# Two fused blocks on one core: mixer operations of Vector with one operand in PSUM, a new order of heads, and a front in a fixed order

## Chip, cores, metric

One core of a Trainium2 chip runs the whole program. The metric is the device time in microseconds (us) of one execution. Five engines work in parallel, each with its own queue in program order: TensorE (PE, matrix products), Vector (DVE), Scalar (ACT), GpSimd (POOL) and SyncE (SP, which here issues most transfers). SBUF is the on-chip memory of the operands, PSUM the memory into which TensorE writes its products.

## What is computed

512 tokens of width 1024 go through two blocks, all in fp32. The first takes `h = rmsnorm(x) * (1 + scale) + shift`, where shift and scale come from a conditioning vector `c` ("ada"), projects h, runs 8 heads of stick-breaking attention and 8 of forgetting attention, and adds a gated output. The second is a mixer, a cross attention to 256 memory rows, and a feed-forward block with a convolution of 3 taps. What the change touches is the start of the program and the mixer, cut from the reference:

```python
def hybrid_mixer(h, ...):                       # second block
    q, k, v, u = split(h @ w_in)                # 4 heads, 2 maps of 64 per head
    q, k = partial_rope(q), partial_rope(k)     # the first 16 of 64 columns turn
    lam = exp(sum(lam_q1 * lam_k1)) - exp(sum(lam_q2 * lam_k2)) + lam_init
    # per head and block of 128 queries:
    p = softmax(where(mask, q @ k.T / 8, -inf)) # both maps
    a = (p[0] - lam * p[1]) @ v
    a = rmsnorm(a, subln_g) * (1 - lam_init)
    c = u[:, :512] * sigmoid(u[:, 512:])
    c = causal_dwconv(c, cv_dw_w) + cv_dw_b     # 31 taps, 512 channels
    c = silu(layernorm(c, cv_ln_g, cv_ln_b))
    return concat([a, c]) @ w_out

def cross_attention(h, m, w_cq, w_ckv, w_co):   # m = rmsnorm(mem, norm_mem_g)
    k, v = split(m @ w_ckv)
```

## The kernel before

Every weight comes in units of 128 x 1024 fp32 (512 KB): `load` (L137) has SyncE transfer it, `split` (L149) has Scalar cast it to a high part `wh` (L152), and Vector or GpSimd subtract that for a low part `wl` (L153); a string of letters D and P says which of the two engines. A product is three matmuls, high by high, high by low and low by high (`mm3`, L159). So a unit feeds 24 matmuls. Three units are buffered.

The order on the engines follows the order in which the program is written, kept by a scheduler that lets an instruction pass another where its model says that this one waits. The written order is in two strings. `FRONT` (L83) mixes the steps of the start: k0 to k7 and v0 to v3 are the products of the memory with `w_ckv` (16 units), n the memory's norm, o the step that multiplies a key product by the norm (L371) and writes it to DRAM (`kv_d`), x the loads of the tokens with their squares (summed by GpSimd into `xacc`, L427), r the norm of the tokens (`row_norm`, L429), a the eight conditioning pairs (`ada`, L409, two Vector operations of 128 x 1024 each), h the normed tokens (`token_h`, L434). Behind h7 come the first block's projections. Sums over the partitions of a column are matmuls with ones (`col_sums`, L238); a reciprocal root is a Scalar root, a Vector reciprocal and four small steps (`rsq_v`, L247); a row of such numbers is spread over the partitions by a cast (`bch`), a subtraction (`bcl`) and matmuls with the identity (`bcast_mm`, L278).

`MIX` (L98) orders the mixer: u is one quarter of the gated input of the convolution (`glu`, L809: two chunks of 24 matmuls), q one half of the heads' queries and keys with their rotation (`rotated`, L858: Scalar copies all columns out of PSUM, then six Vector operations on 64 columns each), v one half of the values, f the front of a head (`diff_front`, L902: scores of both maps, maxima, exponentials, the weighted difference L924), b its back (`diff_back`, L928: transposes, product with v, the head's norm by `rsq_bits`, L258), c one quarter of the convolution (`conv`, L952: 8 taps on TensorE, 14 on Vector in the PSUM bank `sm`, of which there is one, and 9 on Scalar and GpSimd), l the layer norm (L989). Then the output projection runs, first `wo2c` on the convolution (L1036), then `wo2a` on the heads (L1044).

## Time and profile before

| | |
|---|---|
| median of 3 runs | 1317.12 us (1312.56 to 1318.27) |
| the profiled execution | 1315.84 us, of it span 1314.0 |
| TensorE | busy 1229.4 us, 94% of the span |
| Vector | 803.5 us, 61% |
| Scalar | 611.8 us, 47% |
| GpSimd | 472.1 us, 36% |
| mean granted TensorE clock | 0.962 |

The span is what the engines' records cover; the execution lasts 1.84 us longer. A share is a mean over stages with different limits: the busy share of TensorE is near 100% in long stretches and much lower in a few, so the tables by stretch say more than the total. [...]

### The profile page before, as it was taken

The page shows a single profiled execution, that of the slowest core. Times are in us where ns is not written, and L with a number is a line of the kernel's source. Part 1 is how long each engine was busy: PE and PEld are TensorE (multiplying, and loading weights), DVE is VectorE, ACT ScalarE, POOL GpSimd, SP SyncE. Part 2 cuts the span into 40 slices and gives each one's busy share as a digit, 9 for nine tenths or more (in the row PEclk, how much of TensorE's full clock was granted, in tenths as well). Part 3 has the DMA queues.
Part 4 walks back from the last instruction along what each step waited for, and adds up shares of the span by engine and source line. Part 5 has one row for each costly group of instructions (what it writes and reads, how often), then busy time and mean ns, then how long its engine had stood idle before and what let it go on. Part 6 is the DMA issues. An engine that isn't in the chain of part 4 may idle for free.

```text
span 1314.0 us, 16828 instructions
## 1 busy us (share of the span) xinstructions
PE 1229.4 (94%) x6368; PEld 1036.9 (79%) x6368; DVE 803.5 (61%) x1221; ACT 611.8 (47%) x1001; POOL 472.1 (36%) x322
## 2 busy tenths in 40 slices
...
GB/s 362 228 201 124 81 96 73 65 78 92 65 137 257 129 133 98 80 84 94 67 55 41 16 32 144 84 61 48 109 86 101 100 98 99 98 89 88 89 88 65
DMA packets 43715, 135.91 MB, mean 103 GB/s; under 512 B 4977, under 2 KB 8561, under 8 KB 43634
## 3 DMA queue, kind: packets, MB, share of 16 engines
...
HBM read 125.38 MB, written 6.29 MB: 100 GB/s over the span
## 4 chain that ended last, share of the span: by engine, by line
PE 76%; DVE 13%; ACT 4%; issue 3%; DMA 2%; POOL 2%; SPq 0%; DVEq 0%; POOLq 0%; ACTq 0%
PE lin L134 66%; PE z L134 5%; DVE sm L976 2%; PE pv L134 2%; DVE wl L153 1%; PE z L533 1%; DMA wr<-in_wts 1%; DVE ar L413 1%; ACT wh L152 1%; DVE p L924 1%; DVE h L206 1%; POOL wl L153 1%; DVE nm L919 0%; PE sm L134 0%; ACT cpr L972 0%
## 5 line engine op out<-in xcount | busy, mean ns | idle before, releaser
L134 PE MATMUL lin<-h,wh 128*128 128x512 f32 (+1 forms) x2296 | 710.3, 390 | 8.4 <-ACT wh L152 7.9
L134 PEld LDWEIGHTS lin<-h,wh 128*128 128x128 f32 x2296 | 428.7, 191 | 93.3 <-ACT wh L152 10.2
L134 PE MATMUL lin<-h,wl 128*128 128x512 f32 (+1 forms) x1148 | 444.3, 388 | 6.1 <-DVE wl L153 4.4
L153 POOL TENSOR_TENSOR wl<-wr,wh 128x1024 fp32r<-128x1024 f32 (+1 forms) x110 | 268.0, 2436 | 484.0 <-ACT wh L152 455.2
L152 ACT CAST wh<-wr 128x1024 fp32r<-128x1024 f32 (+1 forms) x197 | 204.9, 1042 | 276.5 <-PE lin L134 207.8
L134 PEld LDWEIGHTS lin<-h,wl 128*128 128x128 f32 x1148 | 218.7, 191 | 50.0 <-DVE wl L153 5.6
L153 DVE TENSOR_TENSOR wl<-wr,wh 128x1024 fp32r<-128x1024 f32 (+1 forms) x87 | 115.6, 1328 | 139.8 <-ACT wh L152 139.0
L134 PE MATMUL lin<-wh,h 128*128 128x256 f32 x672 | 128.4, 288 | 2.0 <-ACT wh L152 1.1
L134 PEld LDWEIGHTS lin<-wh,h 128*128 128x128 f32 x672 | 108.0, 195 | 2.6 <-ACT wh L152 1.4
L1158 DVE SCALAR_TENSOR_TENSOR cv<-up,vecs,cv 128x512 f32<-128x512 f32 x88 | 94.5, 1074 | 17.9 <-ACT cv L1156 16.4
L134 PE MATMUL lin<-wl,h 128*128 128x256 f32 x336 | 96.5, 287 | 2.1 <-DVE wl L153 2.1
L134 PE MATMUL lin<-zz,wh 128*128 128x512 f32 (+1 forms) x324 | 92.4, 370 | 0.0
L134 PEld LDWEIGHTS lin<-wl,h 128*128 128x128 f32 x336 | 65.4, 195 | 2.6 <-DVE wl L153 2.4
L134 PEld LDWEIGHTS lin<-zz,wh 128*128 128x128 f32 x324 | 58.5, 188 | 11.4
L134 PE MATMUL lin<-zz,wl 128*128 128x512 f32 (+1 forms) x162 | 60.0, 370 | 0.0
L301 POOL TENSOR_TENSOR nacc<-nacc,sq 128x512 f32<-128x512 f32 x34 | 52.7, 1559 | 14.3 <-ACT sq L300 13.9
L1153 POOL MEMSET up<- 128x2 f32 x44 | 4.3, 99 | 148.8 <-DVE cv L1158 116.7
L604 POOL TENSOR_TENSOR zs<-zs,y 64x512 f32<-64x512 f32 x16 | 26.5, 1654 | 72.2 <-DVE y L603 69.9
L134 PE MATMUL z<-qk 128*128 128x512 f32 (+3 forms) x96 | 36.2, 377 | 8.2 <-ACT p L920 4.9
L976 DVE SCALAR_TENSOR_TENSOR sm<-cp,vecs,sm 128x512 f32<-128x512 f32 x56 | 42.0, 749 | 0.6
L1165 ACT ACTIVATE cv<-cv 128x512 f32<-128x512 f32 x22 | 13.9, 632 | 59.9 <-DVE cv L1158 59.9
L618 DVE TENSOR_TENSOR_SCAN om<-om 128x511 f32<-128x511 f32 (+3 forms) x32 | 36.7, 1187 | 8.2 <-ACT om L614 8.0
(371 smaller groups left out, 1739.4 us busy)
## 6 DMA issues: line engine op xcount, KB each, us to landing
wr<-in_wts SPq DMA_DIRECT2D x197, 512.0 KB, 3.5
...
```

The costliest lines, as they stand in the source:

```text
L134: pe.matmul(o, lhsT=lhsT, rhs=rhs, start=start, stop=stop, skip_group_check=True)
L152: act.copy(out=hi[:, :n], in_=raw[:, :n])
L153: lo_engine().tensor_tensor(out=lo[:, :n], in0=raw[:, :n], in1=f32(hi[:, :n]), op=ALU.subtract)
L206: dve.scalar_tensor_tensor(out=lo, in0=src, scalar=g, in1=f32(hi), op0=ALU.mult, op1=ALU.subtract)
L301: pool.tensor_tensor(out=acc, in0=acc, in1=q, op=ALU.add)
L413: dve.scalar_tensor_tensor(out=r, in0=r, scalar=1.0, in1=cb, op0=ALU.mult, op1=ALU.mult, accum_out=mod[:, 2 * j + n:2 * j + n + 1])
L533: pe.transpose(z[:, o + i * P:o + (i + 1) * P], pt[rb_][:, ro:ro + P], ident)
L604: pool.tensor_tensor(out=zs[r], in0=zs[r], in1=y[r], op=ALU.mult)
L618: dve.tensor_tensor_scan(out=om[:, o:e], data0=om[:, o:e], data1=om[:, o:e], initial=1.0, op0=ALU.mult, op1=ALU.bypass)
L976: dve.scalar_tensor_tensor(out=cz, in0=x_, scalar=w_, in1=cz, op0=ALU.mult, op1=ALU.add)
L1158: dve.scalar_tensor_tensor(out=r, in0=up[:, 2 - j:2 - j + T], scalar=V("ffn_w", c * 3 + j), in1=r, op0=ALU.mult, op1=ALU.add)
L1165: act.activation(out=a, in_=a, func=AF.Silu)
```

## The change

Five edits; the first and the last move instructions.

The front is written in a fixed order for all five engines (`manual_schedule`): a loop over the 16 memory units, each step of which splits unit n + 2, loads what the tables `ADA_LOADS`, `ADA_AT` and `NORM_AT` say, and runs unit n. `START_LO` gives each unit's engine for the low part. The memory's norm no longer scales the products in the front; its numbers (`mrc`, `mrb`) are kept, and the keys and values are scaled when the cross attention reads them back. A token's high and low part are made from a product that reads the norm from PSUM.

The rotation reads q and k from PSUM and leaves its products there, with the norm's factor multiplied into the sine and cosine tables ahead (eight small operations); Scalar copies only the 48 columns that do not turn. In a head's front the exponentials of map 0 go back into PSUM and the difference reads them there; in its back, the steps of the norm and the product with it work in PSUM. The row norm's broadcast `r1b` also stays in PSUM. The string `MIX` is another.

```diff
-START_LO = "DP"
+START_LO = "DDPPDPPDPPDPPDPP"
+ADA_LOADS = (2, 1, 1, 2, 1, 1, 2, 1, 1, 2, 1, 1)
+ADA_AT = (5, 5, 6, 7, 8, 8, 9, 10, 12, 12, 13, 14, 15, 15, 16, 16)
+NORM_AT = (8, 10)
-FRONT = ("k0 k1 n o0 o1 x0 k2 o2 x2 k3 o3 x4 x6 v0 a0 k4 o4 a1 k5 o5 r v1 a2 k6 o6 a3 k7 o7 h0 h1 a4 v2 h2 a5 a6 v3 "
-         "h3 h4 a7 h5 h6 h7")
-MIX = "u0 q0 f0 c0 u1 q1 f1 c1 v1 v0 u2 f3 b0 c2 u3 b1 c3 b3 f2 l b2"
+MIX = "q0 u0 f0 u1 f1 v0 c0 c1 b0 u2 b1 q1 u3 c2 f2 c3 v1 l f3 b2 b3"
...
-    def rsq_bits(o, v):
+    def rsq_bits(o, v, bank):
-        y, t, g = (smp.tile([P, 16], F32, tag="rq" + n, name="rq")[:, :w] for n in "ytg")
+        y = bank[:, 32:32 + w]
+        t, g = (smp.tile([P, 16], F32, tag="rq" + n, name="rq")[:, :w] for n in "tg")
...
-            dve.tensor_tensor(out=t, in0=y, in1=y, op=ALU.mult)
-            dve.tensor_tensor(out=t, in0=t, in1=g, op=ALU.mult)
+            dve.tensor_tensor(out=t, in0=y, in1=g, op=ALU.mult)
+            dve.tensor_tensor(out=t, in0=t, in1=y, op=ALU.mult)
...
+            return lambda: (act.copy(out=q[:, :NM], in_=o),
+                            nc.gpsimd.dma_start(out=kv_d[n // 4, :, (n % 4) * NM:(n % 4 + 1) * NM], in_=q[:, :NM]))
...
     def token_h(j):
-        xk = xt0[:, j]
-        dve.tensor_tensor(out=xk, in0=xk, in1=xrb, op=ALU.mult)
-        act.activation(out=xk, in_=xk, func=AF.Identity, scale=gain[:, j:j + 1], bias=shift[:, j:j + 1])
-        hs.append(split_sb(xk))
+        xk, sh = xt0[:, j], shift[:, j:j + 1]
+        dve.scalar_tensor_tensor(out=xk, in0=xk, scalar=gain[:, j:j + 1], in1=xrb, op0=ALU.mult, op1=ALU.mult)
+        hi, lo = htile(), htile()
+        act.activation(out=hi, in_=xk, func=AF.Identity, bias=sh)
+        dve.scalar_tensor_tensor(out=lo, in0=xk, scalar=sh, in1=f32(hi), op0=ALU.add, op1=ALU.subtract)
+        hs.append((hi, lo))
...
+    with tc.manual_schedule(engines={E_.PE, E_.Activation, E_.DVE, E_.Pool, E_.SP}):
...
+        mem_split(0)
+        load_x(6)
+        mem_split(1)
+        for n in range(17):
+            if n < 16:
+                mem_split(n + 2)
+            if n < len(ADA_LOADS):
+                for _ in range(ADA_LOADS[n]):
+                    ada_load()
+            if n == 0:
+                memory_squares()
+            if 1 <= n <= 4:
+                squares_x(2 * n - 2)
+                squares_x(2 * n - 1)
+            out_ = mem_unit(n) if n < 16 else lambda: None
+            if n == NORM_AT[0]:
+                rsq(xrc, col_sums([xacc]), D)
+                bcast_mm(xrc, xrb)
+            if n == NORM_AT[1]:
+                memory_norm()
+            for i in range(16):
+                if ADA_AT[i] == n:
+                    ada(i)
+                    if i % 2 and n > NORM_AT[0]:
+                        while 2 * len(hs) < i:
+                            token_h(len(hs))
+            out_()
...
-    bcast(r1c, rb[:, 1])
+    r1b = ps_pv()
+    bcast_mm(r1c, r1b)
...
+    for t in (cosb, sinb):
+        for i in range(NT):
+            dve.tensor_scalar(out=t[:, i], in0=t[:, i], scalar1=r12c[:, i:i + 1], scalar2=None, op0=ALU.mult)
...
+            og = o.rearrange("p (a g d) -> p a g d", a=2, d=64)
...
-            dve.tensor_tensor(out=ra, in0=t1, in1=cb, op=ALU.mult)
-            dve.tensor_tensor(out=rb_, in0=t2, in1=sb_, op=ALU.mult)
-            dve.tensor_tensor(out=rc, in0=t2, in1=cb, op=ALU.mult)
-            dve.tensor_tensor(out=rd, in0=t1, in1=sb_, op=ALU.mult)
-            dve.tensor_tensor(out=t1, in0=ra, in1=rb_, op=ALU.subtract)
-            dve.tensor_tensor(out=t2, in0=rc, in1=rd, op=ALU.add)
+            t1, t2 = og[:, :, :, 0:8], og[:, :, :, 8:16]
+            dve.tensor_tensor(out=ta, in0=t2, in1=sb_, op=ALU.mult)
+            dve.tensor_tensor(out=tb, in0=t1, in1=sb_, op=ALU.mult)
+            dve.tensor_tensor(out=t1, in0=t1, in1=cb, op=ALU.mult)
+            dve.tensor_tensor(out=t2, in0=t2, in1=cb, op=ALU.mult)
+            dve.tensor_tensor(out=g[:, :, :, 0:8], in0=t1, in1=ta, op=ALU.subtract)
+            dve.tensor_tensor(out=g[:, :, :, 8:16], in0=t2, in1=tb, op=ALU.add)
...
+                        act.activation(out=zs[0][:, n], in_=zs[0][:, n], func=AF.Exp, bias=nm[:, 0:1],
+                                       accum_out=s0[:, i:i + 1])
...
-                dve.scalar_tensor_tensor(out=s_, in0=s0[:, i:i + 1], scalar=nlam, in1=s_, op0=ALU.mult, op1=ALU.mult)
-                dve.scalar_tensor_tensor(out=pt[b][:, n], in0=pq[b][:, n], scalar=s_, in1=pt[b][:, n],
+                dve.tensor_scalar(out=s_, in0=s_, scalar1=s0[:, i:i + 1], scalar2=nlam, op0=ALU.mult, op1=ALU.mult)
+                dve.scalar_tensor_tensor(out=pt[b][:, n], in0=pq[b][:, n], scalar=s_, in1=zs[0][:, n],
                                          op0=ALU.mult, op1=ALU.add)
...
-        ar = smp.tile([P, T], F32, tag="sq", name="ar")
-        bcast(s0, ar, ps_=ps_lin)
-        dve.tensor_tensor(out=ah, in0=ah, in1=ar, op=ALU.mult)
-        return scaled_split(ah, sg8)
+        b = ps_lin()
+        bcast_mm(s0, b)
+        dve.tensor_tensor(out=b, in0=ah, in1=b, op=ALU.mult)
+        return scaled_split(b, sg8)
...
-        act.copy(out=hi, in_=raw)
-        pool.tensor_tensor(out=lo, in0=raw, in1=f32(hi), op=ALU.subtract)
+        if i < 2:
+            raw4 = raw.rearrange("p (k m) -> p k m", k=4)
+            pool.tensor_tensor(out=raw4, in0=raw4, in1=mrb.unsqueeze(1).to_broadcast([P, 4, NM]), op=ALU.mult)
+            act.copy(out=hi, in_=raw)
+            pool.tensor_tensor(out=lo, in0=raw, in1=f32(hi), op=ALU.subtract)
+        else:
+            act.activation(out=hi, in_=raw, func=AF.Copy, scale=mrc[:, i - 2:i - 1])
+            dve.scalar_tensor_tensor(out=lo, in0=raw, scalar=mrc[:, i - 2:i - 1], in1=f32(hi),
+                                     op0=ALU.mult, op1=ALU.subtract)
```

What the edits move is seen at three places; a row names the line, the operation and output<-inputs. The first is TensorE around the norms in the front. Before, behind the second memory unit: the sums and the broadcast of the memory's norm (`mr`, into `sm`), and the sums of the tokens' norm (`xacc`), with units behind them.

```order
L134 MATMUL sm_227<-ones_86,mr_118 128x1 x2
L134 MATMUL sm_239<-identr_91,bch_240 128x128
L134 MATMUL sm_239<-identr_91,bcl_241 128x128
L134 MATMUL sm_239<-identr_91,bch_240 128x128
L134 MATMUL sm_239<-identr_91,bcl_241 128x128
L243 MATMUL sm_501<-ones_86,xacc_159 128x1 x4
L134 MATMUL lin_301<-h_120,wh_304 128x256
L134 MATMUL lin_301<-h_121,wh_304 128x256
```

Now, at unit 8: the sums of the tokens' norm and, right behind them, its broadcast `xrb`.

```order
L137 MATMUL lin_523<-wh_436,h_143 128x256
L137 MATMUL lin_523<-wl_437,h_143 128x256
L137 MATMUL lin_523<-wh_436,h_144 128x256
L241 MATMUL sm_548<-ones_84,xacc_107 128x1 x4
L137 MATMUL xrb_101<-identr_87,bch_562 128x128
L137 MATMUL xrb_101<-identr_87,bcl_563 128x128
```

Before, units stood between the tokens' sums and the broadcast of their root; now none does. The memory's norm follows two units later in the same way.

The second place is Vector at the first rotation of the mixer. Before, operands and results are `h` and `ro`, both in SBUF:

```order
L871 TENSOR_TENSOR ro<-h,cosb 128x64
L872 TENSOR_TENSOR ro<-h,sinb 128x64
L873 TENSOR_TENSOR ro<-h,cosb 128x64
L874 TENSOR_TENSOR ro<-h,sinb 128x64
L799 SCALAR_TENSOR_TENSOR xr<-xr,vecs,rb 128x512 x8
L875 TENSOR_TENSOR h<-ro 128x8x8
L876 TENSOR_TENSOR h<-ro 128x8x8
L199 TENSOR_TENSOR cpl<-cp,cph 128x542
```

Now the inputs are the bank `lin` in PSUM and one table in SBUF, behind the four scalings of the second table:

```order
L283 TENSOR_TENSOR bcl<-r1c,bch 128x4
L902 TENSOR_SCALAR sinb<-sinb,r12c 128x8 x4
L922 TENSOR_TENSOR ro<-lin,sinb 128x64
L923 TENSOR_TENSOR ro<-lin,sinb 128x64
L924 TENSOR_TENSOR lin<-lin,cosb 128x8x8
L925 TENSOR_TENSOR lin<-lin,cosb 128x8x8
L926 TENSOR_TENSOR h<-lin,ro 128x8x8
L927 TENSOR_TENSOR h<-lin,ro 128x8x8
```

The eight row scalings (`xr`), which stood within the first rotation, are elsewhere now.

The third place is TensorE ahead of the output projection (`wo2c`, whose first product is `lin_7169` before and `lin_7135` now). `lin_7042` is the broadcast of the layer norm, `lin_7144` that of the one head's norm that is left there, and `aq` are the squares of that head:

```order
L134 MATMUL lin_7042<-identr_91,bch_7043 128x128
L243 MATMUL lin_7122<-ones_86,aq_7118 128x1 x4
L134 MATMUL lin_7042<-identr_91,bcl_7044 128x128
L134 MATMUL lin_7042<-identr_91,bch_7043 128x128
L134 MATMUL lin_7042<-identr_91,bcl_7044 128x128
L134 MATMUL lin_7042<-identr_91,bch_7043 128x128
L134 MATMUL lin_7042<-identr_91,bcl_7044 128x128
L134 MATMUL lin_7042<-identr_91,bch_7043 128x128
L134 MATMUL lin_7042<-identr_91,bcl_7044 128x128
L134 MATMUL lin_7144<-identr_91,bch_7145 128x128
L134 MATMUL lin_7169<-h_7057,wh_7165 128x512
```

Now `lin_7030` and `lin_7111` are the broadcasts of two heads' norms; that of the layer norm (`lin_6834`) stands ahead of these rows.

```order
L137 MATMUL lin_6834<-identr_87,bcl_6836 128x128
L137 MATMUL lin_7030<-identr_87,bch_7031 128x128
L241 MATMUL lin_7091<-ones_84,aq_7087 128x1 x4
L137 MATMUL lin_7030<-identr_87,bcl_7032 128x128
L137 MATMUL lin_7030<-identr_87,bch_7031 128x128
L137 MATMUL lin_7030<-identr_87,bcl_7032 128x128
L137 MATMUL lin_7030<-identr_87,bch_7031 128x128
L137 MATMUL lin_7030<-identr_87,bcl_7032 128x128
L137 MATMUL lin_7030<-identr_87,bch_7031 128x128
L137 MATMUL lin_7030<-identr_87,bcl_7032 128x128
L137 MATMUL lin_7111<-identr_87,bch_7112 128x128
L137 MATMUL lin_7135<-h_6849,wh_7131 128x512
```

The sums and the broadcast of one head more stand ahead of the output projection.

## Rows read from the trace of the kernel before

**Rows 1.** The page, busy time of each engine: us, share, instructions.

```profile
PE 1229.4 (94%) x6368; PEld 1036.9 (79%) x6368; DVE 803.5 (61%) x1221; ACT 611.8 (47%) x1001; POOL 472.1 (36%) x322
```

**Rows 2.** Stretches: length, busy time and instructions of each engine, granted clock, DMA share, GB/s.

```profile
60.00:240.00 180.00, 178.94 (x1069) 155.37 (x1067) 110.71 (x133) 97.21 (x160) 83.34 (x58) 1.00 0.38 113
...
521.00:768.00 247.00, 200.84 (x1200) 173.49 (x1199) 186.68 (x349) 128.80 (x237) 113.19 (x69) 0.89 0.20 60
...
640.00:660.00 20.00, 18.50 (x110) 16.25 (x110) 7.76 (x16) 7.98 (x15) 9.05 (x5) 1.00 0.32 104
...
740.00:760.00 20.00, 12.86 (x52) 9.55 (x52) 9.21 (x25) 8.40 (x15) 2.52 (x2) 0.67 0.01 1
```

**Rows 3.** Timeline of TensorE, front: start, us, line, names, count, idle before and releaser.

```profile
10.95 0.79 PE L134 MATMUL lin<-h,wh 128*128 128x256 f32 x2 [2.73 <-ACT wh L152]
...
29.36 0.48 PE L134 MATMUL sm<-identr,bch 128*128 128x128 f32 x1 [5.59 <-ACT bch L282]
...
53.34 0.80 PE L134 MATMUL lin<-h,wh 128*128 128x256 f32 x2 [4.06 <-ACT wh L152]
...
85.69 0.28 PE L134 MATMUL lin<-wl,h 128*128 128x256 f32 x1
...
86.05 0.28 PE L134 MATMUL lin<-wl,h 128*128 128x256 f32 x1
...
86.29 0.63 PE L134 MATMUL lin<-h,wh 128*128 128x512 f32 x2
```

**Rows 4.** Timeline of GpSimd, front.

```profile
11.94 2.46 POOL L355 TENSOR_TENSOR mr<-mr 128x1024 f32<-128x1024 f32 x1 [10.68 <-ACT mr L353]
14.35 2.40 POOL L153 TENSOR_TENSOR wl<-wr,wh 128x1024 fp32r<-128x1024 f32 x1
...
22.14 6.66 POOL L427 TENSOR_TENSOR xacc<-xacc,xq 128x512 f32<-128x512 f32 x5
...
47.02 0.56 POOL L372 DMA_DIRECT2D kv_d<-kvo  x1 [6.90 <-DVE kvo L371]
```

**Rows 5.** The page, groups by cost: busy, mean ns of one, idle before.

```profile
L152 ACT CAST wh<-wr 128x1024 fp32r<-128x1024 f32 (+1 forms) x197 | 204.9, 1042 | 276.5 <-PE lin L134 207.8
```

**Rows 6.** Vector's groups by line and shape, 540 to 780 us.

```profile
L976 DVE SCALAR_TENSOR_TENSOR sm<-cp,vecs,sm 128x512 f32<-128x512 f32 x56 | 42.0, 749 | 0.6
...
L799 DVE SCALAR_TENSOR_TENSOR xr<-xr,vecs,rb 128x512 f32<-128x512 f32 x8 | 9.7, 1276 | 0.0
...
L923 DVE SCALAR_TENSOR_TENSOR smc<-s,nlam,smc 128x1 f32<-128x1 f32 x16 | 7.1, 442 | 1.9 <-ACT p L921 1.8
...
L924 DVE SCALAR_TENSOR_TENSOR p<-p,smc 128x512 f32<-128x512 f32 x4 | 5.2, 1301 | 0.1
```

**Rows 7.** One stretch, only the instructions of the rotation (tile `ro`): length, Vector's busy time.

```profile
540.00:780.00 240.00, 34.63 (x48) 0.87 0.18 54
```

**Rows 8.** Timeline of Vector in the mixer.

```profile
534.98 2.37 DVE L283 TENSOR_TENSOR bcl<-r12c,bch 128x4 fp32r<-128x4 f32 x1 [1.12 <-ACT bch L282]
...
606.65 2.44 DVE L876 TENSOR_TENSOR h<-ro 128x64 f32<-128x64 f32 x1
...
615.35 0.21 DVE L871 TENSOR_TENSOR ro<-h,cosb 128x64 f32<-128x64 f32 x1
```

**Rows 9.** Timeline of GpSimd in the mixer.

```profile
606.59 2.42 POOL L153 TENSOR_TENSOR wl<-wr,wh 128x1024 fp32r<-128x1024 f32 x1
```

**Rows 10.** Timeline of Vector at the mixer's end.

```profile
731.08 0.15 DVE L939 SCALAR_TENSOR_TENSOR s<-lin,s 128x4 f32<-128x4 f32 x1
...
737.78 0.15 DVE L938 SCALAR_TENSOR_TENSOR s<-s 128x4 f32<-128x4 f32 x1
```

**Rows 11.** Timeline of TensorE: the mixer's first matmul, its last convolution, the output projection.

```profile
521.14 0.61 PE L134 MATMUL lin<-h,wh 128*128 128x512 f32 x2
...
724.60 0.39 PE L134 MATMUL sm<-cph,wl 128*128 128x512 f32 x1
...
767.65 1.16 PE L134 MATMUL lin<-h,wh 128*128 128x512 f32 x2
```

245 lines of the change are left out of this document (126 added, 119 removed).

## The prediction

> **What bounds the kernel now.** I read the busy times first: TensorE is busy for 94% of the span [rows 1], so a gain can only come out of the stretches in which it waits or runs at the lower clock. The table of stretches finds them. From 60 to 240 us TensorE has no slack to speak of, 178.94 us of 180 [rows 2]. Two places are different. The first is the front, before the token projections. Its sixteen memory units are 24 matmuls each, and at full clock three matmuls take 0.36 us (85.69 to 86.05 in [rows 3]), so a unit takes 2.88 us and all sixteen 46.1. They run from 10.95 to 86.29 [rows 3], which is 75.3: 29 us are lost, in single waits of 5.59 and 4.06 us and in the half clock behind them (a 128-column matmul takes 0.48 us at 29.36).
>
> The second is the mixer. Its first matmul is at 521.14 and the output projection behind it begins at 767.65 [rows 11]: 246.5 us. In that stretch TensorE is busy for 200.84 us at a mean granted clock of 0.89, and Vector for 186.68 [rows 2]. So 46 us are waits. The work itself, at the pace of rows 3 (0.12 us for 256 columns, twice that for 512), is 69 us for the six halves of q, k and v, 44 for the eight u chunks, 22 for four convolutions and about 41 for scores, transposes, values, sums and the layer norm: 176. The other 24 us of the 200.84 are lost to the clock. It matters where these 70 us lie. Between 640 and 660 Vector is busy for only 7.76 us [rows 2]: its backlog from the first half is worked off by then, beside dense matmuls that hardly waited. The loss comes behind it, where little dense work is left (740 to 760: TensorE 12.86 us at clock 0.67). From the end of the last convolution at 725.0 to 767.65 another 42.7 us pass [rows 11].
>
> **The front.** In the new order every queue is fixed, and GpSimd sets the pace up to unit 8. Its first sum can start at 11.94 [rows 4] plus one or two casts of 1.04 [rows 5] that now stand ahead of the squares: I take 13.5. Ahead of unit 8 stand the memory sums (2.46 for the first, half and a quarter of it for the others: 4.3), seven additions of squares at 1.33 (9.3), five low parts at 2.40 (12.0) and five transfers at 0.56 (2.8) [rows 4]: 28.4, so 41.9, and unit 8 ends at 44.8. Then TensorE issues the row sums and, with no unit in between, the broadcast that needs their root. The same chain for the memory norm cost 5.59 before [rows 3]; in it was the kind of stretched operation that rows 8 show (2.37 us for four columns), and without one it would be 3.2. I take 4.5. Units 9 and 10 (5.8) and the memory norm, placed the same way (4.5), end at 59.6. Vector then has tokens 0 to 3 ahead of unit 13's low part: each is two Vector operations and a Scalar one, all of 512 columns, taken at 0.75 us by [rows 6], 9.0 in all if they go one after another. Units 11 and 12 (5.8) run beside that; unit 13 starts near 70.5, and three units later, at 79 to 80, the projections begin. Before they began at 86.29: **6 us** gained, which TensorE's full queue behind it keeps [rows 2]. At best (cheap norms, tokens hidden) 76, a gain of 10; with both chains stretched to 5.6 and the clock down behind each, 86, no gain.
>
> **Vector in the mixer.** The trace shows why its small operations are dear. A rotation operation of 64 columns takes 0.21 us at 615.35, issued 0.14 behind one another, and 2.44 at 606.65, where GpSimd started a 2.42 us subtraction at 606.59 [rows 8, 9]. The convolution's 56 taps, with one operand in PSUM, run at 749 ns [rows 6] and show nothing of it, although GpSimd worked beside many of them. The edits give the affected operations one PSUM operand. The 48 rotation operations go from 34.6 us [rows 7] to 48 times 0.14, 6.7; the eight row scalings from 1276 ns to about 700 (4.6 saved); the sixteen one-column factors from 442 to about 160 (4.5); the map products, 1301 ns at full width, to 0.75 (6 over all widths); the norms' small steps perhaps 1.5 a head (6). Eight new scalings of the cosine and sine tables cost 0.2 each by the uncontended row [rows 8], and stand where the first heads wait for a broadcast anyway. Together near 49 us of 187.
>
> [...]
>
> [...]
>
> **What of it reaches the end.** Most of the 34.6 us lay before 640, beside a busy TensorE, and nobody waited for it. The gain depends on the new order, which spreads the dense work. I add four stretches. (A) q, k half 0, u0, u1, front 0, v0: 63 us of dense work, and waits of 3: 66. (B) convolutions 0 and 1, front 1, backs 0 and 1, u2. The accumulator has one bank, so the second convolution waits until Vector has added the 14 taps of the first (14 times 0.75, 10.5), which share it with front 1 (9 to 10): 5.6 + 20 + 6 for the second, 12 for u2, 12 for the norm chain of back 1, whose broadcast stands ahead of q half 1 on TensorE: 56, with about 24 of waits. (C) q, k half 1, u3, convolution 2, v1, front 2: 54 of work, 56. (D) Vector's backlog of taps and front 2, convolution 3, its taps beside front 3, the layer norm with the norms of heads 2 and 3 on TensorE ahead of the output: 20 plus the 42.7 of before: 63. Sum 241 against 246.5: **6 us** (5.5) gained. Bounds: if B's waits vanish under u2, and the clock stays up, 216 to 222; if front 3 delays the last taps, 254.
>
> **The memory's keys and values** take their norm later: two GpSimd multiplications of 2.4 us each stand in for two low parts that go to Vector, and four low parts become two. Nothing on the path; plus or minus 1.5, should the first key be late. Sum: 1315.84 - 6 - 6 = 1303.8. The median of the runs is 1.3 above the profiled execution, so **1305**.
>
> **Rivals.** (1) TensorE becomes the bound in the mixer. With 49 us less on Vector, backs and fronts end under dense work, and only the tail of 42.7 us, in which some 13 us are work, is left to wait: 176 + 30, and 10 to 15 for the clock and the single accumulator: about 219, that is 27 less, with the front about 1285. For it: Vector at 138 us of 241 would be far from full. Against: the waits in B and D are chains, not load. (2) The saved Vector time stays beside a busy TensorE, and the fixed front only moves its waits from splits to norms: B and D cost what the old second half did, and the front gains 2 to 4: 1314. For it: Vector's idle stretch at 640 [rows 2]. (3) Slower: both norms of the front stall TensorE with nothing put in between, at 5.6 and with half clock for a unit behind each (2.9 more): the projections start at 88; and in the mixer front 3's row maxima and products (7 us of Vector, by the widths of rows 6) queue ahead of convolution 3's taps, so that everything behind comes 8 later: 1327. It decides if front 3 is issued on Vector before the taps. The order puts the scores of front 3 right behind that convolution on TensorE, which speaks for it; the taps need no scores, which speaks against. (4) The edits don't do what they say: PSUM operands are stretched too. Then rotations stay near 35 us, and the result is that of (2).
>
> **How the numbers follow.** My forecast, 0.46 (own range 1294 to 1311); rival 1, 0.20; rivals 2 and 4 together, 0.22; rival 3, 0.12. A measurement here tells a change from none at about 0.5%, 6.6 us: 1310.5 to 1323.7 is the same. Faster: most of the forecast (0.42), rival 1 (0.20) and a little of rival 2 (0.02): 0.64. Slower: most of rival 3, 0.09. Same: 0.27. The range for 8 in 10 leaves out the upper half of rival 3 and the lower part of rival 1: 1282 to 1320.
>
> **What would show it.** In the changed profile the first 512-column projection should start near 80, with two waits of 4 to 5 us for a broadcast at about 45 and 55 us; the rotation operations should be near 0.2 us with GpSimd working; from the mixer's first matmul to the output projection some 241 us. I am wrong if rotations still show 1 to 2.4 us, if TensorE waits in the front for splits and not for norms, or if the mixer's second half has no waits for taps and norm broadcasts.

## The result and the profile after

The changed kernel takes 1327.46 us (median of 5 runs, 1323.88 to 1329.81) where the kernel before takes 1315.65 (5 runs, 1312.56 to 1318.27): a ratio of 1.0090 with an interval of 1.0064 to 1.0116. It is 11.8 us slower. The prediction was 1305 us, faster; its range ended at 1320. Direction and time were both wrong.

The profiled execution took 1326.44 us, its span 1324.7. The page's busy times answer to [rows 1]:

```profile
PE 1240.5 (94%) x6368; PEld 1048.1 (79%) x6368; DVE 754.4 (57%) x1215; ACT 603.6 (46%) x994; POOL 483.6 (37%) x326
```

Vector has 49 us less to do in the whole program. The prediction had that sum for the mixer alone, and that the two agree is chance: up to the output projection the mixer saves 43 (below), and the front 11, which the prediction had not counted. TensorE, with the same 6368 matmuls, is busy 11 us longer: its waits did not grow in total (84.2 us of the span against 84.6), but more of its work ran at the lower clock (the mean granted clock, as a share of the full one, is 0.955 against 0.962). The stretches show where. The columns are those of [rows 2]; the third row is the mixer up to the output projection, the last two lie in its tail:

```profile
60.00:240.00 180.00, 170.86 (x966) 146.03 (x965) 116.07 (x156) 95.86 (x163) 85.06 (x59) 0.98 0.36 111
525.00:778.00 253.00, 207.60 (x1199) 181.31 (x1197) 144.05 (x354) 125.03 (x235) 112.07 (x69) 0.83 0.20 59
740.00:760.00 20.00, 12.83 (x46) 10.14 (x44) 9.76 (x17) 7.66 (x13) 2.52 (x2) 0.50 0.00 0
760.00:780.00 20.00, 10.64 (x44) 9.79 (x45) 11.77 (x45) 7.65 (x14) 0.00 (x0) 0.50 0.00 1
```

From 60 to 240 us, where TensorE had no slack before, 9 us are missing now: the front's waits have moved past 60, and there are some up to 107. In the mixer Vector works 43 us less than before (144.05 against 186.68), yet the stretch is 253 us long instead of 247, and its mean clock is 0.83 instead of 0.89.

Since both kernels have the same number of matmuls, they can also be laid beside each other by count. The start of the n-th matmul, taken from the records of TensorE (microseconds; the third kernel is an experiment told below):

```
n      what it is                      before   after  (diff.)   y68_lo_keep (diff. to before)
186    a memory unit                    53.34   40.80  -12.54      36.34  -17.00
234    (sums of the tokens' norm, new)  63.25   51.08  -12.17      45.90  -17.35
306    a memory unit                    71.89   65.62   -6.27      60.48  -11.41
426    behind all memory units          86.29   87.19   +0.90      82.63   -3.66
606    first projections               113.03  116.98   +3.95     112.43   -0.60
2706   start of the mixer              521.14  525.22   +4.08
3936   output projection               776.96  786.36   +9.40
4106   behind the memory's k and v     815.49  828.09  +12.60
6367   last                           1306.98 1317.63  +10.65
```

So the loss has three places: 4 us in the front, 5.3 in the mixer, 3.2 where the memory's keys and values are read back. The front is the odd one: at matmul 186 it is 12.5 us ahead, and it gives all of that back by 426. (The 2 us regained at the end lie where nothing was changed, and the front alone, experiment 5, does not regain them: I put no weight on them.)

Each column is one execution. Ten kernels here have the old front, and they reach matmul 426 at 86.25 to 88.16 us and matmul 606 at 112.98 to 114.90; the two with the new front (the changed kernel and experiment 5) reach 426 at 87.19 and 88.05, and 606 at 116.98 and 117.94. So up to 426 no loss can be told, and at 606 it is 2 to 5 us. The stretch between the two is sharper: 26.7 us in all ten, 29.8 and 29.9 in the two.

**What the operands did.** The rotation's instructions on the tile `ro` took 34.63 us over 48 instructions [rows 7]. Of those that still use it, in the same stretch:

```profile
540.00:780.00 240.00, 4.88 (x28) 0.82 0.19 55
```

And two of Vector's groups there (line, operands, count, busy, mean ns of one):

```profile
L922 DVE TENSOR_TENSOR ro<-lin,sinb 128x64 f32<-128x64 f32 x7 | 1.6, 225 | 21.4 <-ACT h L916 21.4
L983 DVE SCALAR_TENSOR_TENSOR p<-p,smc,z 128x512 f32<-128x512 f32 x4 | 3.0, 740 | 0.0
```

A rotation step takes 225 ns. GpSimd was idle beside the seven steps of the first row; steps that ran beside a GpSimd instruction took as little, 0.23 and 0.21 us in experiment 2. All 48 steps together (L922 to L927) keep Vector busy for 8.7 us, where the prediction had 6.7, and the map product fell from 1301 to 740 ns [rows 6]. The edit does what the prediction said of it. The 21.4 us in the first of these rows are Vector's own waits for Scalar: Vector is now early there.

**The front.** TensorE's waits (start, us, line, names, count, wait and releaser), and the start of the norm's sums:

```profile
25.22 0.58 PE L137 MATMUL lin<-h,wl 128*128 128x256 f32 x1 [3.81 <-POOL wl L156]
...
38.06 0.39 PE L137 MATMUL lin<-h,wl 128*128 128x256 f32 x1 [1.75 <-POOL wl L156]
...
46.73 0.39 PE L137 MATMUL lin<-wl,h 128*128 128x256 f32 x1 [2.04 <-POOL wl L156]
...
51.08 0.94 PE L241 MATMUL sm<-ones,xacc 128*128 128x1 f32 x8
...
53.74 0.33 PE L137 MATMUL xrb<-identr,bch 128*128 128x128 f32 x1 [1.72 <-ACT bch L282]
...
64.70 0.47 PE L137 MATMUL sm<-identr,bch 128*128 128x128 f32 x1 [2.08 <-ACT bch L282]
...
98.26 0.38 PE L137 MATMUL z<-wh,h 128*128 128x256 f32 x1 [1.58 <-DVE xt L445]
```

The three longest before the norm are all for GpSimd's low parts, as the prediction had it; the two norm waits are short. The wait at 98.26 is for a token (L445), inside the projections, where the prediction had counted on cover. How the lateness at 46.73 arises is seen on the other engines:

```profile
14.75 2.41 POOL L156 TENSOR_TENSOR wl<-wr,wh 128x1024 fp32r<-128x1024 f32 x1 [14.30 <-ACT wh L155]
...
32.44 2.68 POOL L440 TENSOR_TENSOR xacc<-xacc,xq 128x512 f32<-128x512 f32 x2
...
35.64 2.36 POOL L156 TENSOR_TENSOR wl<-wr,wh 128x1024 fp32r<-128x1024 f32 x1
37.96 3.55 POOL L440 TENSOR_TENSOR xacc<-xacc,xq 128x512 f32<-128x512 f32 x2
...
44.34 2.34 POOL L156 TENSOR_TENSOR wl<-wr,wh 128x1024 fp32r<-128x1024 f32 x1 [0.20 <-ACT wh L155]
```

```profile
35.65 4.69 DVE L156 TENSOR_TENSOR wl<-wr,wh 128x1024 fp32r<-128x1024 f32 x1 [12.69 <-ACT wh L155]
```

```profile
41.52 0.29 ACT L426 ACTIVATE shift<-mod,vecs 128x1 f32<-128x1 f32 x1 [5.90 <-DVE ar L424]
...
43.21 1.05 ACT L155 CAST wh<-wr 128x1024 fp32r<-128x1024 f32 x1
```

GpSimd and Vector start a low part at the same instant (35.64), both with two operands in SBUF. Vector's takes 4.69 us, where such a one takes 1.23 on its own, and it overlaps the two additions behind GpSimd's subtraction, which take 3.55 us where the pair before took 2.68. Vector's conditioning pair comes behind it, Scalar's one-column shift waits 5.90 us for that pair, and the cast of unit 8, next in Scalar's queue, waits behind the shift. Unit 8's low part on GpSimd waits for the cast.

**The memory's keys and values.** All engines, around the second key (L1133) and the first value (L1136):

```profile
817.65 3.54 DVE L1136 SCALAR_TENSOR_TENSOR kvl<-wr,mrc,kvh 128x1024 fp32r<-128x1024 f32 x1 [0.48 <-ACT kvh L1135]
...
817.67 2.44 POOL L1133 TENSOR_TENSOR kvl<-wr,kvh 128x1024 fp32r<-128x1024 f32 x1
...
821.11 1.75 DVE L209 SCALAR_TENSOR_TENSOR h<-xr,vecs,h 128x512 fp32r<-128x512 f32 x1
...
822.79 0.68 DVE L1113 TENSOR_TENSOR xr<-lin,xr 128x512 f32<-128x512 f32 x1
...
823.52 0.73 PE L137 MATMUL lin<-h,wh 128*128 128x512 f32 x2 [2.09 <-DVE xr L1113]
```

The change takes such pairs of operands out of the mixer, and puts two new ones on Vector here. The value's low part takes 3.54 us beside GpSimd's; behind it stands the instruction that empties the output projection's bank (L1113), and TensorE waits 2.09 us for the bank. With the front alone (5) the same low part takes 3.52 us and the same wait is 2.08.

### The profile page after: what moved, and what is told of

Its sections match the earlier page's. It is cut to its first block, busy times and chain, and to the rows that moved or that the text cites. A ratio compares the mean times of both kernels' runs of the same rounds, so it can differ in the third digit from the quotient of the medians.

```text
span 1324.7 us, 16821 instructions
## 1 busy us (share of the span) xinstructions
PE 1240.5 (94%) x6368; PEld 1048.1 (79%) x6368; DVE 754.4 (57%) x1215; ACT 603.6 (46%) x994; POOL 483.6 (37%) x326
## 5 line engine op out<-in xcount | busy, mean ns | idle before, releaser
L156 POOL TENSOR_TENSOR wl<-wr,wh 128x1024 fp32r<-128x1024 f32 (+1 forms) x115 | 278.5, 2423 | 508.2 <-ACT wh L155 454.9
L156 DVE TENSOR_TENSOR wl<-wr,wh 128x1024 fp32r<-128x1024 f32 (+1 forms) x82 | 110.6, 1349 | 138.2 <-ACT wh L155 137.6
L137 PE MATMUL lin<-wh,h 128*128 128x256 f32 x672 | 133.4, 294 | 1.6 <-ACT wh L155 1.6
L137 PEld LDWEIGHTS lin<-wh,h 128*128 128x128 f32 x672 | 111.9, 201 | 2.1 <-ACT wh L155 2.0
L1038 DVE SCALAR_TENSOR_TENSOR sm<-cp,vecs,sm 128x512 f32<-128x512 f32 x56 | 42.0, 750 | 14.5 <-PE sm L137 13.5
```

The costliest lines, as they stand in the source:

```text
L137: pe.matmul(o, lhsT=lhsT, rhs=rhs, start=start, stop=stop, skip_group_check=True)
L156: lo_engine().tensor_tensor(out=lo[:, :n], in0=raw[:, :n], in1=f32(hi[:, :n]), op=ALU.subtract)
L1038: dve.scalar_tensor_tensor(out=cz, in0=x_, scalar=w_, in1=cz, op0=ALU.mult, op1=ALU.add)
```

## Where in the mixer

To compare kernels whose mixers start at different times, I cut each into three: from its first matmul to the first convolution, on to the end of the last convolution, and on to the end of both output products. Before:

```profile
521.00:559.00 38.00, 38.00 (x278) 36.03 (x276) 26.25 (x43) 19.25 (x30) 24.51 (x13) 1.00 0.27 81
559.00:725.00 166.00, 140.56 (x825) 120.29 (x824) 130.53 (x225) 89.99 (x166) 83.02 (x53) 0.92 0.23 67
725.00:827.00 102.00, 79.71 (x342) 63.53 (x342) 63.69 (x114) 45.44 (x73) 38.71 (x21) 0.83 0.21 67
```

After:

```profile
525.00:590.00 65.00, 65.00 (x454) 59.92 (x453) 31.44 (x90) 36.66 (x64) 34.01 (x19) 1.00 0.28 85
590.00:726.00 136.00, 112.77 (x628) 97.52 (x627) 77.52 (x173) 66.00 (x125) 75.54 (x49) 0.85 0.22 65
726.00:838.00 112.00, 85.63 (x358) 68.78 (x357) 71.50 (x123) 45.01 (x77) 36.33 (x17) 0.79 0.19 60
```

The new order puts 65 us of dense products ahead of the first convolution instead of 38. They run without a wait and at full clock, and Vector is needed for half of that stretch. The 27 us of dense work are then missing behind it: the middle still has 23 us of waits (25 before), though Vector does there only 77.52 us of work where it did 130.53, and the tail is 10 us longer.

## Experiments

The first three runs do one part of the change alone; a fourth leaves the front out. The times are medians, with the kernel before timed on the same chip. For several kernels I give, in us from the first matmul of the mixer, when the convolutions' sums (taps included) were ready, when the last convolution ended, when the first output product began and when both had ended; then TensorE's waits in that time and the time at half clock, all from the records:

```
kernel               sums of the convolutions     conv. 3  output  both    waits  half
                     0      1      2      3       ended    began   ended          clock
before               69.8  120.1  167.7  222.4    203.8    246.5   306.1   47.7   61.4
e1_ops               60.6  107.2  161.1  212.4    195.5    237.4   296.4   39.4   61.4
e10_rot              64.0  107.6  157.9  211.4    192.8    235.2   293.6   40.4   54.6
e2_order             94.4  116.6  189.9  218.6    197.8    251.2   310.4   52.1   68.3
e4_ops_order         92.9  115.8  193.2  221.2    200.8    251.5   310.6   48.9   81.9
after                91.9  114.0  193.0  221.4    201.1    252.9   313.0   49.6   88.7
e11_out_first        92.9  115.7  193.1  221.0    200.7    240.9   316.9   52.5   85.3
e12_early_old_ops    64.6   99.1  128.1  156.6    142.9    208.0   289.1   31.5   44.4
c5_early_norm2       56.4   89.3  120.8  145.4    132.1    202.8   281.4   26.4   44.4
c6_early_norm3       56.4   89.3  119.2  145.4    131.1    208.0   293.1   35.9   54.6
c3_early_norm        56.4   89.3  116.1  143.5    130.0    213.7   301.0   39.8   61.4
```

**1. The operands alone** (rotation, map difference, norms, row scaling; order and front as before):

```diff
-            dve.tensor_tensor(out=ra, in0=t1, in1=cb, op=ALU.mult)
...
+            dve.tensor_tensor(out=ta, in0=t2, in1=sb_, op=ALU.mult)
...
-                dve.scalar_tensor_tensor(out=pt[b][:, n], in0=pq[b][:, n], scalar=s_, in1=pt[b][:, n],
+                dve.scalar_tensor_tensor(out=pt[b][:, n], in0=pq[b][:, n], scalar=s_, in1=zs[0][:, n],
```

> The kernel before with the PSUM operands of the mixer alone (rotation, difference, norms, row scaling); the front and the order of heads are those of before. Theory A (Vector's saving lies beside a busy TensorE, the order of heads costs the time through waits without dense work and a lower clock): Vector's busy time in the mixer falls from 187 to about 145 us, the 4.90 us wait for the rotation at 571 goes, TensorE's other waits stay; 1309 to 1314 us, 2 to 6 below before. Theory B (operands in PSUM hold banks longer, and that is what the change pays for): TensorE waits more for free banks, 3 to 8 us slower than before, 1319 to 1324.

Measured: 1305.06 us against 1316.19, ratio 0.9912 (0.9889 to 0.9934), 11.1 faster, more than either theory gave. In the old order the operands are worth 11 us. The middle stretch shrinks from 166 to 157 us; TensorE waits 17 us in it where it waited 25:

```profile
563.00:720.00 157.00, 139.84 (x822) 120.99 (x821) 93.42 (x223) 89.58 (x169) 79.95 (x51) 0.90 0.23 70
```

**2. The rotation alone** (added to see how much of that is the rotation):

```diff
-            dve.tensor_tensor(out=ra, in0=t1, in1=cb, op=ALU.mult)
...
+            dve.tensor_tensor(out=ta, in0=t2, in1=sb_, op=ALU.mult)
+            dve.tensor_tensor(out=tb, in0=t1, in1=sb_, op=ALU.mult)
+            dve.tensor_tensor(out=t1, in0=t1, in1=cb, op=ALU.mult)
```

> The kernel before with the rotation's edit alone (it reads q and k from PSUM, the tables carry the norm's factor); all else as before. The operands together gave 11.1 us in the old order. If it is the rotation on Vector's queue ahead of the convolution's taps in the first half (the first convolution ends 9 us after its start earlier with all operands, the second 13): 1305 to 1309, 7 to 10 below before, with the first convolution's sum ready 60 to 62 us after the mixer's start (69.9 before). If the difference and the norms at the end give it: 1312 to 1316.

Measured: 1306.11 us against 1316.10, ratio 0.9924 (0.9903 to 0.9944), 10.0 faster: it cannot be told apart from the whole of the operands. Vector's timeline shows the way. Before, the rotations of the second, third and fourth pair of blocks stand ahead of the taps of the first convolution and are stretched; the taps (L976) start at 572.70 and the sum is ready (L978) at 590.98:

```profile
556.20 2.44 DVE L876 TENSOR_TENSOR h<-ro 128x64 f32<-128x64 f32 x1
...
572.70 2.34 DVE L976 SCALAR_TENSOR_TENSOR sm<-cp,vecs,sm 128x512 f32<-128x512 f32 x3
...
590.30 0.68 DVE L978 TENSOR_TENSOR ca<-sm,rb 128x512 f32<-128x512 f32 x1
```

With the rotation alone changed, each pair takes 1.2 us, and the same sum is ready 5.8 us earlier in the mixer (64.0 instead of 69.8), though this mixer began 2.9 us later:

```profile
566.53 0.23 DVE L881 TENSOR_TENSOR h<-lin,ro 128x64 f32<-128x64 f32 x1
566.67 0.21 DVE L882 TENSOR_TENSOR h<-lin,ro 128x64 f32<-128x64 f32 x1
...
569.20 2.34 DVE L982 SCALAR_TENSOR_TENSOR sm<-cp,vecs,sm 128x512 f32<-128x512 f32 x3
...
587.32 0.68 DVE L984 TENSOR_TENSOR ca<-sm,rb 128x512 f32<-128x512 f32 x1
```

The two steps shown ran beside GpSimd's additions, which read their operands from SBUF, and took 0.23 and 0.21 us:

```profile
563.02 4.04 POOL L979 TENSOR_TENSOR rb<-rb,cpr 128x512 f32<-128x512 f32 x3
```

By the second sum the convolutions are 12.5 us ahead. TensorE itself had waited only once for a rotation, before:

```profile
571.38 0.46 PE L883 MATMUL z<-idf,h 128*128 128x128 f32 x2 [4.90 <-DVE h L876]
```

The gain is twice that wait, so part of it came through Vector's queue; the two shares were not measured apart.

**3. The order alone:**

```diff
-MIX = "u0 q0 f0 c0 u1 q1 f1 c1 v1 v0 u2 f3 b0 c2 u3 b1 c3 b3 f2 l b2"
+MIX = "q0 u0 f0 u1 f1 v0 c0 c1 b0 u2 b1 q1 u3 c2 f2 c3 v1 l f3 b2 b3"
```

> The kernel before with the new order of heads alone. Theory A: the order is what costs; with Vector still slow the waits of the two convolutions in a row and of the two norms at the end are longer than in the changed kernel: 1322 to 1330, 6 to 14 slower than before, with more than 80 us of the mixer at half clock (56 before). Theory B: the order is harmless, 1312 to 1318.

Measured: 1321.31 us (9 runs) against 1316.19, ratio 1.0039 (1.0027 to 1.0051), 5.1 slower, just below the range of theory A, and with 68.3 us of the mixer at half clock, not more than 80. The prediction had taken the order as what would turn Vector's time into a gain. The order by itself also shortens the rotation steps: with their old operands the 48 of them take 16.65 us here, not 34.63. That fewer of them lie beside GpSimd is my reading; no row shows it:

```profile
521.00:780.00 259.00, 16.65 (x48) 0.87 0.19 57
```

**4. Operands and order, with the old front** (the diffs of 1 and 3 together):

> The kernel before with the PSUM operands and the new order of heads together, front and memory norm as before. Alone, the operands gave 11.1 us and the order cost 5.1. If the two add up: 1310, 6 below before. If the new order leaves Vector's saved time without use (its waits are chains and its loss is clock): the changed kernel less its front and its later memory norm (5.9), that is 1321, 5 above before.

Measured: 1320.00 us against 1314.48, ratio 1.0040 (1.0026 to 1.0054), 5.5 slower. In the new order the operands are worth nothing that can be measured, where they are worth 11 in the old. Compared with the order alone, the waits fall by 3.2 us and the time at half clock grows by 13.6 (table). Vector in the first stretch of the order alone, and of operands and order:

```profile
521.00:586.00 65.00, 37.86 (x80) 1.00 0.28 84
```

```profile
523.00:588.00 65.00, 31.76 (x90) 1.00 0.28 85
```

Vector is idle for 42 and 51% of the dense stretch in which the first rotations lie. Nobody waits for them there. The operands also have less left to save: over the three stretches of the mixer Vector's time falls by 20.6 us in the new order (197.6 to 177.0), by 46.2 in the old (220.5 to 174.3). How much of the lost gain each of the two accounts for was not measured apart.

**5. The front and the later norm of the memory, alone:**

```diff
-FRONT = ("k0 k1 n o0 o1 x0 k2 o2 x2 k3 o3 x4 x6 v0 a0 k4 o4 a1 k5 o5 r v1 a2 k6 o6 a3 k7 o7 h0 h1 a4 v2 h2 a5 a6 v3 "
...
+    with tc.manual_schedule(engines={E_.PE, E_.Activation, E_.DVE, E_.Pool, E_.SP}):
...
+            act.activation(out=hi, in_=raw, func=AF.Copy, scale=mrc[:, i - 2:i - 1])
```

> The kernel before with the new front alone (with the memory's norm applied later). By the two traces, matched matmul by matmul, the front costs 4.0 us (0.7 until the projections start, 3.2 in waits inside the first projections): 1319 to 1320. If the front's loss came only together with the other edits: 1314 to 1317.

Measured: 1322.08 us (8 runs) against 1316.19, ratio 1.0047 (1.0030 to 1.0065), 5.9 slower, 2 more than expected; by count of matmuls it is 4.9 us late at 606 and loses 3.2 more at the memory's keys and values. With 5.5 for operands and order that makes 11.4 of the 11.8 that the whole change costs. The three parts taken singly (-11.1, +5.1, +5.9) would have made nothing: they do not add up, because the operands' gain is gone under the new order.

**6. A mend in the front and one at the memory's values.** Scalar's shifts and gains are issued behind the next cast, and the memory's values are scaled in place by Scalar, so that their low parts can go back to GpSimd:

```diff
-            act.activation(out=shift[:, j:j + 1], in_=m, func=AF.Identity, bias=V("b_shift", j))
+            late.append(lambda: act.activation(out=shift[:, j:j + 1], in_=m, func=AF.Identity, bias=V("b_shift", j)))
...
-            act.activation(out=hi, in_=raw, func=AF.Copy, scale=mrc[:, i - 2:i - 1])
-            dve.scalar_tensor_tensor(out=lo, in0=raw, scalar=mrc[:, i - 2:i - 1], in1=f32(hi),
-                                     op0=ALU.mult, op1=ALU.subtract)
+            act.activation(out=raw, in_=raw, func=AF.Copy, scale=mrc[:, i - 2:i - 1])
+            act.copy(out=hi, in_=raw)
+            pool.tensor_tensor(out=lo, in0=raw, in1=f32(hi), op=ALU.subtract)
```

> The changed kernel with two edits that touch different stages, read apart in the trace matmul by matmul. First, Scalar's two small shift and gain operations of a conditioning pair are issued one step later, behind the next unit's cast. If they hold that cast back on Scalar's queue (5.9 us of idle time before the first shift, the cast of unit 8 right behind it), unit 8 starts 2 to 3 us earlier and the first projections too; if GpSimd's list is the bound, nothing moves by more than 1. Second, the memory's values are scaled in place by Scalar and their low parts go back from Vector to GpSimd: if Vector's low part of 3.54 us beside GpSimd is what made the cross attention's queries wait 2.09 us, the 3.2 us lost behind the output projection fall to under 1; if the added multiplications on GpSimd cost it, they stay. Both right: 1321 to 1323; both wrong: 1327 to 1329.

Measured: 1334.27 us against 1314.48, ratio 1.0152 (1.0136 to 1.0168): slower than the changed kernel itself, and outside every range of the expectation. The sums of the tokens' norm begin 3.0 us earlier (48.09 instead of 51.08), as the first theory had it, but at matmul 306 only 0.9 of that is left, and the 1.2 at 606 (+2.80 instead of +3.95) lie within what one kernel's front varies by: the waits moved. At the keys and values it loses 6.0 us where the changed kernel loses 3.2, and 5.3 more soon behind. GpSimd is loaded there too, and Vector's own instructions then meet it:

```profile
822.90 2.79 POOL L1143 TENSOR_TENSOR kvl<-wr,kvh 128x1024 fp32r<-128x1024 f32 x1
...
824.01 2.76 DVE L156 TENSOR_TENSOR wl<-wr,wh 128x1024 fp32r<-128x1024 f32 x1
...
826.83 0.80 PE L137 MATMUL z<-h,wl 128*128 128x512 f32 x1 [3.96 <-DVE wl L156]
```

So the low parts are no cheaper on GpSimd, at least with the extra pass on Scalar that this edit puts ahead of them. The run does not tell what Vector's long low part costs from what the scaling costs as such: that the 3.2 us come through Vector's queue rests on the rows above, with their wait of 2.09 us.

**7. GpSimd's list, and the clock in the tail.** Low parts of units 3 and 6 go to Vector; and 22 matmuls (not 17, as the expectation says) whose result nobody uses are added in the layer norm, to keep TensorE working:

```diff
-START_LO = "DDPPDPPDPPDPPDPP"
+START_LO = "DDPDDPDDPPDPPDPP"
...
+            mm(keep, ones, cacc[c], True, True)
...
+                mm(keep, y2c[-1][0][:, :P], y2c[-1][0], True, True)
```

> The changed kernel with two edits in different stages. First, the low parts of memory units 3 and 6 go from GpSimd to Vector, which idles for 12.7 us there. If GpSimd's list sets the front, the waits of 3.81 and 1.75 us for its low parts go and the projections start 4 to 5 us earlier; if Scalar's queue does, 0 to 2. Second, 17 further matmuls, whose results nobody reads, fill TensorE's waits in the layer norm at the mixer's end; they compute nothing of the output. If the lower clock there is the cost (47.8 us at half clock), it comes back to full within the layer norm, and mixer start to output projection falls from 252.9 to 247 to 250 us; if the chains on Vector and Scalar set the end, it stays at 252 to 255. Both right: 1318 to 1321; both wrong: 1327 to 1330.

Measured: 1323.23 us against 1314.48, ratio 1.0058 (1.0035 to 1.0081), 4.2 less than the changed kernel. The two intervals overlap (the other is 1.0064 to 1.0116), so the traces have to say whose it is. It is the front's: the norm's sums begin 5.2 us earlier,

```profile
45.90 1.03 PE L241 MATMUL sm<-ones,xacc 128*128 128x1 f32 x8
```

which is 51.08 in the changed kernel, and matmul 606 starts 4.55 us earlier, which is more than fronts of one kernel differ by. GpSimd's list did set the pace up to unit 8. The matmuls that were added raised the clock in part, and saved no time. TensorE in 46 us of the tail, after and here (busy, clock):

```profile
733.00:779.00 46.00, 25.89 (x95) 0.50 0.00 1
```

```profile
729.00:775.00 46.00, 33.26 (x115) 0.63 0.00 1
```

From the mixer's start to the output projection it is 254.0 us here and 252.9 there, and both outputs have ended at 312.9 and 313.0. A quarter of the lost clock came back and the length stayed, which speaks for the chains on Vector, Scalar and GpSimd as what sets it. At full clock the tail was not seen, so a share of the clock in it is not excluded.

**8. The output of the convolution ahead of the last heads' norms.** In the tail of the changed kernel TensorE waits for one norm after another, first the layer norm, then two heads' norms. Before, one head's norm was left there, with the same wait of 4.87 us (at 767.38); the second one, from 771.43 to the output's first product at 778.15, makes 6.7 of the 9.1 us by which this tail is longer:

```profile
759.31 1.86 PE L137 MATMUL lin<-ones,cpr 128*128 128x1 f32 x8 [2.12 <-POOL cpr L1063]
...
771.43 0.47 PE L137 MATMUL lin<-identr,bch 128*128 128x128 f32 x1 [4.87 <-ACT bch L282]
...
777.88 0.47 PE L137 MATMUL lin<-identr,bch 128*128 128x128 f32 x1 [2.77 <-ACT bch L282]
```

The prediction had named the norms of heads 2 and 3 there. On operands and order (4), the output of the convolution becomes two steps w0, w1 of the string, put ahead of the last backs:

```diff
-MIX = "q0 u0 f0 u1 f1 v0 c0 c1 b0 u2 b1 q1 u3 c2 f2 c3 v1 l f3 b2 b3"
+MIX = "q0 u0 f0 u1 f1 v0 c0 c1 b0 u2 b1 q1 u3 c2 f2 c3 v1 l f3 w0 w1 b2 b3"
```

> The PSUM operands and the new order with the old front, and the convolution's output products issued ahead of the norms of heads 2 and 3. With those norms ahead of them, last convolution to output took 51.8 us, 9.1 more than before, and TensorE waited 4.87 and 2.77 us for their broadcasts. If this is what costs the new order its time: last convolution's end to first output product falls to 41 to 44 us and the time from 1320.0 to 1309 to 1313. If the chain behind the last convolution (taps beside front 3, layer norm) is the cost whatever stands behind it: 1317 to 1320.

Measured: 1325.91 us against 1316.10, ratio 1.0088 (1.0061 to 1.0115): slower than either case of the expectation. The output does begin 10.6 us earlier (240.9 instead of 251.5), but both outputs end 6.3 later (316.9 instead of 310.6): the heads' norms then wait at the end with nothing beside them (3.88 and 2.78 us at 790.71 and 797.17). Neither place of this dense work covers both chains.

**9. Convolutions early, dense work spread.** If the dense products are what is missing, they should lie beside the chains and the convolutions should start early. An order of this kind, with w0, w1 as in 8, operands as in the change and the old front:

```diff
-MIX = "u0 q0 f0 c0 u1 q1 f1 c1 v1 v0 u2 f3 b0 c2 u3 b1 c3 b3 f2 l b2"
+MIX = "u0 q0 c0 u1 f0 c1 u2 f1 c2 u3 v0 c3 q1 b0 l v1 b1 f2 f3 w0 b2 w1 b3"
```

> The old front, the PSUM operands, and a third order (u0 q0 c0 u1 f0 c1 u2 f1 c2 u3 v0 c3 q1 b0 l v1 b1 f2 f3, then the convolution's output in two parts between b2 and b3), to see whether dense products beside the norms give more than the old order does. In the order with early convolutions the mixer was 6 to 9 us shorter than before, the old order with the same operands 9.8. If dense work beside the layer norm is what is missing: 1296 to 1303. If the number of short waits stays, wherever they lie: 1305 to 1313.

Measured: 1291.50 us against 1314.48, ratio 0.9829 (0.9815 to 0.9843): 23 us faster than the kernel before, 4.5 below the expected range, and the fastest of all runs here. Its three stretches:

```profile
524.00:562.00 38.00, 38.00 (x275) 36.02 (x275) 18.63 (x50) 19.70 (x32) 27.57 (x17) 1.00 0.27 82
562.00:656.00 94.00, 91.46 (x519) 78.92 (x517) 66.47 (x133) 58.62 (x107) 67.69 (x44) 0.98 0.27 84
656.00:806.00 150.00, 126.12 (x660) 106.53 (x658) 95.04 (x201) 71.63 (x130) 50.23 (x27) 0.86 0.22 67
```

The middle has 2.5 us of waits instead of 23 to 25. The last convolution ends at 132 us of the mixer, so that q half 1, v half 1 and half of the output are left as cover for the layer norm and the heads.

The same order without the operands' edits:

```diff
-            t1, t2 = og[:, :, :, 0:8], og[:, :, :, 8:16]
+            t1, t2 = g[:, :, :, 0:8], g[:, :, :, 8:16]
```

> The kernel before with the order of the run at 1291.5 us, with Vector's operands as before (none in PSUM). If Vector's queue is near the bound in that order: 10 to 20 us slower than with the operands, 1301 to 1312. If the order alone gives it: 1290 to 1296.

Measured: 1301.62 us against 1316.10, ratio 0.9893 (0.9875 to 0.9911), 14.5 faster by the order alone. The operands give another 0.6% in this order, about 8 us (the difference of the two ratios).

Two neighbours show how narrow this is. Both have back 0 ahead of q half 1 and back 1 ahead of v half 1; the first also has the last quarter of the convolution ahead of v half 0, and front 2 ahead of v half 1:

```diff
+MIX = "u0 q0 c0 u1 f0 c1 u2 f1 c2 u3 c3 v0 b0 q1 l b1 f2 v1 f3 w0 b2 w1 b3"
...
+MIX = "u0 q0 c0 u1 f0 c1 u2 f1 c2 u3 v0 c3 b0 q1 l b1 v1 f2 f3 w0 b2 w1 b3"
```

> The old front, the PSUM operands, and another order: all u and convolutions early (u0 q0 c0 u1 f0 c1 u2 f1 c2 u3 c3 v0 b0 q1 l b1 f2 v1 f3 then the output of the convolution in two parts between b2 and b3), so that the layer norm lies beside the dense q and v products and the output's products beside the last heads. If the mixer's loss is waits without dense work beside them (theory A), its 46 us of waits shrink by 20 to 30 and the half clock with them: 1285 to 1300. If the chains of the norms and the single accumulator bank set the time whatever stands beside them: 1308 to 1318.

> The order of the run at 1291.5 us with back 0 ahead of q half 1 and back 1 ahead of v half 1, so that these chains get dense products beside them earlier. From 680 to 700 us TensorE was busy for 13.7 of 20 us there at clock 0.67. If that stretch can be filled: 1284 to 1290; if the filling only moves the wait: 1291 to 1296.

The first took 1312.27 us (10 runs, 1306.59 to 1319.90) against 1316.19, ratio 0.9976 (0.9953 to 0.9999), as its second theory had it; the second, which differs from the best only in b0 standing ahead of q1 and b1 ahead of v1, 1304.55 against 1316.10, ratio 0.9903 (0.9877 to 0.9928), above both cases of its expectation. It ends the last convolution as early as the best (131.1), and loses 12 us behind it, 9.5 of them in waits. From 704 to 714 us TensorE waits three times, 1.89, 1.99 and 6.16 us, with no dense product beside: in that time Vector and Scalar have front 2, the layer norm, back 1's norm and the queries of front 3 to do. The longest:

```profile
714.05 0.77 PE L134 MATMUL z<-qk 128*128 128x512 f32 x1 [6.16 <-DVE rq L270]
```

The profile puts this wait down to a step of the norm (`rq`); the transfer of those queries, issued at 711.63 with some 2.3 us to landing, ends there too. The best order has no wait above 3.9 us behind its last convolution. So backs ahead of the dense halves are worse than behind them. The three orders end the last convolution alike, at 130 to 132 us, and both outputs at 281, 293 and 301: early convolutions alone do not make the gain, the place of the dense work behind them counts as well.

## Why the prediction was wrong, by its steps

Between the sum of 1303.8 and the profiled execution of 1326.44 lie 22.6 us. By the count of matmuls the mixer has about 11 of them (+5.3 for -5.5), the front 10 (+4 for -6) and the memory's keys and values 3; the 2 regained at the end go off.

**"Most of the 34.6 us lay before 640, beside a busy TensorE, and nobody waited for it."** This is the step that failed first. The rotation's time was mostly beside a busy TensorE, and yet its removal alone gave 10 us (2). What I read from the busy share was that TensorE had no wait there; the trace of before has one, of 4.90 us at 571.38. Beside it the taps of the first convolution stood behind the rotations in Vector's queue, and by my reading dense work was used up meanwhile which is missing later: the idle Vector at 640 to 660 [rows 2] came some 70 us too late to help. A helper's time beside a busy TensorE costs nothing only if what it delays is not needed by the time when the dense work runs out.

**The new order, taken as 241 against 246.5 us.** It costs 5.1 by itself (3) and cancels the operands' 11 (4). Of the four terms, A was right: 65.3 us to the first convolution where I had 66. B ended, where q half 1 begins, at 124.4 (649.6 in the trace) where I had 122. C and D together took 128.5 where I had 119: that is the mis-sized term. I gave D the old tail of 42.7 us with two heads' norms in it; from the end of the last convolution to the output it is 51.8 now, and 6.7 of these 9.1 us are the second head's norm (8). And I did not ask what A pays for: 27 us of dense work more than before, ahead of the first convolution.

**The front, taken as -6.** It is +4 in this trace (2 to 5 by the spread of the other fronts). The list of GpSimd ahead of unit 8 was the right bound (7), but unit 8 ended at 51.1, not at 44.8. Of these 6.3 us, 1.25 are a later start (14.75 for 13.5), 0.9 the seven additions (10.2 for 9.3, the pair beside Vector's low part), 0.7 a sixth transfer, 1.8 GpSimd's waits for Scalar's copy and cast behind that shift, 0.2 the memory sums, and 1.5 unit 8 itself (4.35 us from 46.73, at a mean clock of 0.60). From there to 65.6 the two norms and the units between them took 14.5 us, where I had 14.8: those terms held (the 4.5 for the first norm was 4.3, from 51.08 to the unit at 55.37: sums, a wait of 1.7 and the broadcast). From there to the end of the last memory unit it is 21.6 instead of 19.9. The last piece is the stretch behind the units (matmul 426 to 606): I gave what is left of the tokens there no cost, and 3.05 us are lost, of which the waits at 98.26, 106.16 and 107.29 are 2.5. Only the first of these (1.58) is for a token; the other two (0.28 and 0.63) are for the high and the low part of a weight. In (7), with the front 4.6 earlier, the same 3.05 are lost.

**The memory's keys and values, "plus or minus 1.5".** They cost 3.2, in the whole change and in the front alone (5). I had seen that two low parts go to Vector and did not apply to them what I had just read from rows 8 and 9: with two operands in SBUF a rotation step took 2.44 us beside a GpSimd subtraction, and 0.21 without. That this is the whole of the 3.2 is not shown; with these low parts on GpSimd (6) the loss is greater.

**What was right.** The operands' edits, in mechanism and nearly in size: 43 us less of Vector in the mixer for 49, a rotation of 8.7 us for 6.7, one-column factors at 266 ns for 160. The 49 itself had left out the eight new scalings, 1.6 us at 0.2 each. Rotation steps with one operand in PSUM took 0.23 and 0.21 us beside GpSimd's additions in (2); the low parts that keep two operands in SBUF took 4.69 and 3.54 us beside its subtractions. Whether the new scalings, with all operands in SBUF, would be stretched as well is not shown: four of them took 0.63 us together (536.60), but GpSimd had nothing to do then; the one-column factor of a head's front (L982) took 0.27 us beside GpSimd (586.72) as without it (575.25). No price of a source in PSUM shows: 0.21 to 0.23 us for a rotation step with one operand in PSUM, 0.21 for an uncontended one without [rows 8], and 0.15 us each for a step of the norm that reads PSUM and its neighbour that does not [rows 10].

**The rivals.** The time of the third, 1327, was met, and neither of its mechanisms: the norm waits of the front were 1.7 and 2.1 us, not 5.6, and the last taps were ready 20.3 us behind the last convolution where it was 18.6 before, not 8 later. The second rival, that the saved time stays beside a busy TensorE, is what the new order does and the old one does not. Of the signs of being wrong that the prediction named, one came: TensorE waited in the front for splits (3.81, 1.75 and 2.04 us ahead of the norm) more than for norms.

**What stays open.** Which of the moved steps in the new order costs most; why the time at half clock grew by 13.6 us between (3) and (4) while the waits fell, and what of it cost time outside the tail, since only the tail was tried with added matmuls; and whether the new order loses by its late convolutions, by its early dense work or by both, which no run changes singly.
